# A chunked state-space scan beside a large projection: new state in three rounded products, state update first on VectorE, none of the scan on GpSimd

## The chip, the cores and the metric

The kernel runs on one core of one Trainium2 chip. The metric is the device time of one execution in microseconds (us); the kernel before was timed three times, and its median is 2664.36 us. About 0.2%, some 5 us, is what a timing of this kernel can tell from no change.

A core has several engines with instruction queues of their own: TensorE for matrix products (its weight loads are listed apart, as PEld), VectorE (DVE in the rows), ScalarE (ACT), GpSimd (POOL) and SyncE (SP), whose queue here issues the DMA transfers. Each engine works through its queue in order, and an instruction that has to wait holds up those behind it.

## The reference

One layer of a hybrid encoder on 2048 positions of width 1024, float32 throughout: RMSNorm, one input projection, two token mixers side by side (a gated short convolution and a Mamba-2 scan), an output projection with a residual, RMSNorm, a squared-ReLU MLP of width 4096 with a residual, and a last RMSNorm. The part that matters here is the scan:

```
x_c    = xs * dt                                  # per head
scores = einsum("bclgn,bcsgn->bclsg", c_c, b_c)
y_diag = einsum("bclsgr,bcsgrp->bclgrp", scores * decay, x_c)
states = einsum("bclgn,bclgrp->bcgrpn", b_c, x_c * decay_end)
h      = h_before * chunk_decay + states          # from chunk to chunk
y_off  = einsum("bclgn,bcgrpn->bclgrp", c_c, h_before) * exp(a_cum)
y      = rmsnorm_per_group((y_diag + y_off + d_skip * xs) * silu(z))
```

There are 16 heads of 64 in 2 groups, with a state of 128 per group.

## The kernel before

**Products.** Nearly all products are made of three products of rounded parts. A float32 array is split into `hi`, its copy rounded to the type fp32r, and `lo`, the rest (array minus `hi`, rounded as well); `mm3` issues whi·hi, whi·lo and wlo·hi into one PSUM bank. A split is a cast on ScalarE and a subtraction on VectorE (`split_w`, L100 and L101, for weights; L1422 and L1423 for the mixers' outputs). The small products of the scan are made in plain float32 instead; the trace has two records for each of these.

**Stages.** First the input projection runs on the first half of the positions, then on the second half; its products are `chain` (L276 to L278). From the second half on the scan runs as a side job: 32 chunks of 128 positions by one group (4 blocks of 512 positions, 2 groups, 4 chunks each), the first 16 beside the second half of the input projection and the last 16 beside the output projection. Then come the MLP and the last norm, which the change does not touch.

**The scan.** `Scan` gives each chunk a front and a back, generators whose steps `run` deals out. `front` transposes x and B (L1253, L1255) and makes the scores (L1256) on TensorE, copies the transposes out on ScalarE (L1258 `xtok`, L1260 `btok`), masks the scores (L1262), makes the decays on ScalarE (L1267, L1268), weights x by dt and by the decay to the end (`xdt` and `xde`, L1273) and multiplies decay by scores (L1275). `back` makes on TensorE the old state's part `yo` (L1287, 4 products), the new state `st` (L1289, one product of 512 columns) and the diagonal part `yd` (L1292, 8 products); then on VectorE `yo` times its decay (L1301), the state's decay (L1302), the addition of `st` to the state (L1303) and of `yd` (L1304); then on GpSimd the skip term (L1307) and the gate (L1308); then the group norm: squares on ScalarE (L1311), sums (L1312, L1314), a product with ones (L1317), a root (L1319), a reciprocal (L1320), a scaling (L1322), and the DMA to the scratch tensor `yn_d` (L1323).

**Buffers.** The two transposes, `st` and (in the first 16 chunks) the norm's sums take turns on two PSUM banks, tag "tp". So the transpose of B for the next chunk (`ptb`, L1255) takes the bank that `st` of this chunk had, and cannot start before L1303 has read it. `yo` and `yd` have a bank each. In the last 16 chunks the norm's sums take turns with the squares of the output projection (`sq`, L1491, read by L1492) on another single bank. `xtok` and `btok` have one buffer, `stmp` three in the first 16 chunks and four in the last.

**The output projection.** `Output` has 64 units; each is 24 products into one bank (L113 to L115), a residual addition on VectorE (L1478) and a DMA out (L1479). Units 0 to 31 use the short convolution's output, 32 to 47 the scan's output of blocks 0 and 1, 48 to 63 that of blocks 2 and 3, where block 3 is first used in unit 50. `schedule` lists at which half unit (`at` is 2n in the middle of unit n, 2n+1 at its end) a block of mixer output is fetched (L1408) and at which it is split into places (L1421 to L1423). The function `hook` runs in units 0 to 44 three steps of the scan a unit and whatever `todo` lists for that half unit. The scan's 134 steps are all dealt out when unit 44 ends. From unit 48 another `hook` deals out the preparation of the MLP's input.

**Order.** What is written is a priority, not the order on an engine: the framework plans every engine's queue with a model of durations, takes the first written instruction that its model says is ready, and fixes that order. In the trace L1302 comes before L1301 in some chunks and L1304 before L1303 in others. Instructions far ahead in the text run as soon as their data and buffers are there by the model.

Of the kernel before, what the change touches and what calls it, by code (L numbers as in the profile page):

```python
# [11 lines left out]
F32 = mybir.dt.float32  # L12
F32R = mybir.dt.float32r
AF = mybir.ActivationFunctionType
ALU = mybir.AluOpType

P = 128
# [22 lines left out]
def trunk(ctx: ExitStack, tc: tile.TileContext, x, w_in, w_dt, w_out, w_up, w_down, cvec, hrow, out):  # L40
    nc = tc.nc
# [38 lines left out]
        out=tri, in_=tri, compare_op=ALU.is_ge, fill=0.0, base=0, pattern=[[1, P]], channel_multiplier=-1  # L80
# [4 lines left out]
    def col(base, i):  # L85
        return cv[:, base + i : base + i + 1]
# [25 lines left out]
    def mm3(out, whi, wlo, hi, lo, k, nk):  # L112
        nc.tensor.matmul(out, whi, hi, start=(k == 0), stop=False)  # L113
        nc.tensor.matmul(out, whi, lo, start=False, stop=False)  # L114
        nc.tensor.matmul(out, wlo, hi, start=False, stop=(k == nk - 1))  # L115

    def psum(tag, name, bufs=1):
        if tag in turns:
            tag = next(turns[tag])
        return ps.tile([P, 512], F32, tag=tag, name=name, bufs=bufs)  # L120
# [1060 lines left out]
    class Scan:  # L1181
# [63 lines left out]
        def front(self, n):  # L1245

            b, g, c, h, ts, r0 = self.place(n)
            t = self.got[n]
            bT, cT = t["bc"][:, 0], t["bc"][:, 1]
            byhead = lambda a: a.rearrange("p (h d) -> p h d", h=HG)  # L1250
            pt = psum("tp", "ptx", 2)
            for j in range(4):
                nc.tensor.transpose(pt[:, j * P : (j + 1) * P], t["xd"][:, j], ident)  # L1253
            pb = psum("tp", "ptb", 2)
            nc.tensor.transpose(pb[:, 0:P], bT, ident)  # L1255
            nc.tensor.matmul(pb[:, P : 2 * P], bT, cT, start=True, stop=True)  # L1256
            xtok = self.tile([512], "xtok", 1)
            nc.scalar.copy(xtok, pt)  # L1258
            btok = t["btok"] = self.tile([P], "btok", 1)
            nc.scalar.copy(btok, pb[:, 0:P])  # L1260
            sm = self.tile([L], "smask", 1)
            nc.vector.tensor_tensor(out=sm, in0=pb[:, P : 2 * P], in1=tri, op=ALU.mult)  # L1262
            yield

            dec = t["dec"]
            for i in range(HG):
                nc.scalar.activation(dec[:, i], dec[:, i], AF.Relu, bias=t["a"][:, i : i + 1], scale=-1.0)  # L1267
            nc.scalar.activation(dec, dec, AF.Exp, scale=-1.0)  # L1268
            for j in range(4):
                nc.scalar.mul(t["xd"][:, j], t["xd"][:, j], col(C_D, 4 * g + j))  # L1270
            for k, by in (("xdt", "dt"), ("xde", "dend")):
                t[k] = self.tmp()
                nc.vector.tensor_tensor(out=byhead(t[k]), in0=byhead(xtok), in1=t[by], op=ALU.mult)  # L1273
            yield
            nc.vector.tensor_tensor(out=dec, in0=dec, in1=sm.unsqueeze(1).to_broadcast([P, HG, L]), op=ALU.mult)  # L1275
            yield

        def back(self, n):

            b, g, c, h, ts, r0 = self.place(n)  # L1280
            t = self.got.pop(n)
            cT = t["bc"][:, 1]
            byhead = lambda a: a.rearrange("p (h d) -> p h d", h=HG)
            state = self.state[g]
            yo = psum("k4", "yo")
            for j in range(4):
                nc.tensor.matmul(yo[:, j * L : (j + 1) * L], state[:, j * P : (j + 1) * P], cT, start=True, stop=True)  # L1287
            st = psum("tp", "st", 2)
            nc.tensor.matmul(st, t["btok"], t["xde"], start=True, stop=True)  # L1289
            yd = psum("k5", "yd")  # L1290
            for i in range(HG):
                nc.tensor.matmul(  # L1292
                    yd[(i % 2) * 64 : (i % 2) * 64 + 64, (i // 2) * L : (i // 2 + 1) * L],
                    byhead(t["xdt"])[:, i, :],
                    t["dec"][:, i, :],
                    start=True,
                    stop=True,
                )
            y = t["y"]
            t1 = self.tmp()  # L1300
            nc.vector.tensor_tensor(out=t1, in0=yo, in1=t["eb"].rearrange("p j l -> p (j l)"), op=ALU.mult)  # L1301
            nc.vector.tensor_tensor(out=byhead(state), in0=byhead(state), in1=t["cdec"], op=ALU.mult)  # L1302
            nc.vector.tensor_tensor(out=state, in0=state, in1=st, op=ALU.add)  # L1303
            nc.vector.tensor_tensor(out=t1, in0=t1, in1=yd, op=ALU.add)  # L1304
            yield
            t3 = t1.rearrange("p (j l) -> p j l", j=4)
            nc.gpsimd.tensor_tensor(out=t3, in0=t3, in1=t["xd"], op=ALU.add)  # L1307
            nc.gpsimd.tensor_tensor(out=y, in0=t3, in1=y, op=ALU.mult)  # L1308
            yield
            q4 = self.tmp().rearrange("p (j l) -> p j l", j=4)  # L1310
            nc.scalar.activation(q4, y, AF.Square)  # L1311
            nc.vector.tensor_tensor(out=q4[:, 0:2], in0=q4[:, 0:2], in1=q4[:, 2:4], op=ALU.add)  # L1312
            ssq = self.tile([L], "ssq", 1)
            nc.vector.tensor_tensor(out=ssq, in0=q4[:, 0], in1=q4[:, 1], op=ALU.add)  # L1314
            yield
            pss = psum("tp", "pss", 2) if self.bufs == 1 else psum("mw", "pss")
            nc.tensor.matmul(pss[:, 0:L], ones, ssq, start=True, stop=True)  # L1317
            r = self.tile([L], "srstd", 1)
            nc.scalar.activation(r, pss[:, 0:L], AF.Sqrt, bias=eps, scale=1.0 / 512)  # L1319
            nc.vector.reciprocal(out=r, in_=r)  # L1320
            yield
            nc.vector.tensor_tensor(out=y, in0=y, in1=r.unsqueeze(1).to_broadcast([P, 4, L]), op=ALU.mult)  # L1322
            nc.sync.dma_start(yn_d[h][:, 4 * g : 4 * g + 4, ts], y)  # L1323
            yield

        def run(self, begin, end):
# [10 lines left out]
            if self.bufs == 1:  # L1337
                for n in range(begin, end):
                    back = self.back(n)
                    front = self.front(n + 1) if n + 1 < end else iter(())  # L1340
                    next(back)
                    yield
                    next(back)
                    self.load(n + 1)
                    self.load_rows(n + 1)
                    yield
                    next(back)
                    yield
                    yield
                    next(front, None)  # L1350
                    yield
                    next(back)
                    yield
                    next(front, None)
                    yield
                    next(back)
                    self.load_gate(n + 1)
                    yield
                    next(front, None)
                    yield  # L1360
                return
# [28 lines left out]
    class Output:  # L1390
# [103 lines left out]
        def schedule(self):  # L1494

            self.todo = {}
            held = {}

            def put(i, b, c, load, splits):
                def fetch():  # L1500
                    held[i, b] = [self.fetch(i, b, k, self.raw) for k in range(0, KD, 2)]

                self.todo.setdefault(load, []).append(fetch)
                for j, at in enumerate(splits):
                    self.todo.setdefault(at, []).append(lambda j=j: self.fill(i, b, c, 2 * j, held[i, b][j]))

            put(0, 2, 2, 2, (5, 7, 9, 11))
            put(0, 3, 0, 26, (30, 30, 31, 31))
            put(1, 0, 1, 34, (38, 40, 42, 44))
            put(1, 1, 2, 58, (62, 62, 63, 63))  # L1510
            put(1, 2, 0, 68, (72, 74, 76, 78))
            put(1, 3, 1, 90, (94, 94, 95, 95))


    c4 = ctx.enter_context(ExitStack())
    with ExitStack() as c1:
# [7 lines left out]
        proj_out = Output(proj.places)  # L1524
# [10 lines left out]
        with ExitStack() as c2:  # L1535
            scan.open(c2, "sp2", 2)
            side = scan.run(len(CHUNKS) // 2, len(CHUNKS))

            def hook(at):
                for _ in range(1 + at % 2):  # L1540
                    next(side, None)
                for f in proj_out.todo.pop(at, ()):
                    f()

            for n in range(45):
                proj_out.unit(n, hook)
            for _ in side:
                pass
            for n in range(45, 48):
                proj_out.unit(n, hook)  # L1550
        c5.close()
        mlp = Mlp()
        mlp.raws = c4.enter_context(tc.tile_pool(name="ur", bufs=1, side="right", reuse_waits="tile"))
# [8 lines left out]

        def hook(at):
            next(late, None)
            if at == 2 * 61 + 1:
                mlp.settle(mlp.places, 0, [t[0] for t in mlp.held])

# [75 lines left out]
```

## Time and profile before

| | |
|---|---|
| timed runs | 2661.9, 2664.36 and 2666.43 us |
| the profiled execution's own time | 2658.11 us |
| its span | 2656.4 us |
| mean granted TensorE clock | 0.995 of full |
| busy: TensorE, weight loads | 2602.2 us, 2124.8 us |
| busy: VectorE, ScalarE, GpSimd | 1874.3 us, 1436.5 us, 146.1 us |
| scan's first 16 chunks | 470 to 980 us of the span, about |
| scan's last 16 chunks | 980 to 1295 us, about |

Busy time of TensorE counts pipelined products with ends that are modelled, so the cost of a product is read from start to start of the products around it, not from its own duration. Times in rows are from the start of the span. A row of an engine's idle time names what ended it.

### The profile page before, as it was taken

Reading aid. Unit: us, or ns where it says so; the run is one execution under the profiler, and the core shown is the slowest. Engines: PE = TensorE matmul, PEld = TensorE weight load, DVE = VectorE, ACT = ScalarE, POOL = GpSimd, SP = SyncE. Lnnn points to the kernel's source line nnn. Section 1 sums busy time; section 2 is a strip of 40 time slices with the busy share of each in tenths; the row PEclk is TensorE's granted clock in tenths of the full one; section 3 lists DMA queues with packets and bytes.
Section 4 is the critical chain, followed back from the end, with each engine's and each line's share of the span. In section 5 each row is a group of like instructions: output and inputs, shape, how many; then the busy total and the mean of one; then the engine's idle time right before and its main releaser. Section 6 shows DMA issues by size and latency. Waiting matters only on the chain.

```text
span 2656.4 us, 33528 instructions
## 1 busy us (share of the span) xinstructions
PE 2602.2 (98%) x12024; PEld 2124.8 (80%) x12024; DVE 1874.3 (71%) x2524; ACT 1436.5 (54%) x2178; POOL 146.1 (6%) x162
## 2 busy tenths in 40 slices
PE   7999999999999999998999999999999999999998
PEld 5788888778877888776888888888887888888887
DVE  7977867667667666666678675744447877888985
ACT  6654345766567566857336555755555434444443
POOL 0010000111111001111000000000000000000001
PEclk9999999999999999999999999999999999999999
DMA  3545735555555578867566786765558554665762
GB/s 145 196 174 182 278 143 202 182 152 174 169 161 168 165 262 267 254 200 232 193 208 214 258 315 254 258 234 178 209 183 297 155 152 153 206 219 165 249 209 71
DMA packets 292871, 536.96 MB, mean 202 GB/s; under 512 B 26208, under 2 KB 141920, under 8 KB 292704
## 3 DMA queue, kind: packets, MB, share of 16 engines
q1 hardware_dynamic: 292704, 534.82, 60.9%
q8 instruction: 94, 1.54, 0.2%
q14 instruction: 73, 0.60, 0.1%
HBM read 354.89 MB, written 179.83 MB: 201 GB/s over the span
## 4 chain that ended last, share of the span: by engine, by line
PE 59%; issue 26%; ACT 5%; DMA 4%; DVE 4%; POOL 1%; SPq 0%; POOLq 0%; DVEq 0%; ACTq 0%
PE px L276 9%; PE px L277 9%; PE px L278 9%; PE py L276 4%; PE py L277 4%; PE py L278 4%; PE pm L113 4%; PE pm L114 4%; PE pm L115 3%; PE pw L276 2%; PE pw L277 2%; PE pw L278 2%; ACT whi L100 1%; ACT dec L1267 1%; DMA dec<-rd_d 1%
## 5 line engine op out<-in xcount | busy, mean ns | idle before, releaser
L276 PE MATMUL px<-uh,whi 128*128 128x512 f32 x1672 | 657.7, 393 | 6.8 <-DVE acc L1018 1.8
L278 PE MATMUL px<-uh,wlo 128*128 128x512 f32 x1672 | 652.2, 390 | 0.0
L277 PE MATMUL px<-ul,whi 128*128 128x512 f32 x1672 | 651.9, 390 | 0.0
L276 PEld LDWEIGHTS px<-uh,whi 128*128 128x128 f32 x1672 | 314.5, 188 | 82.2 <-DVE acc L1018 3.2
L101 DVE TENSOR_TENSOR wlo<-wraw,whi 128x1024 fp32r<-128x1024 f32 x214 | 223.2, 1043 | 222.2 <-ACT whi L100 216.4
L278 PEld LDWEIGHTS px<-uh,wlo 128*128 128x128 f32 x1672 | 314.4, 188 | 66.4 <-issue 0.2
L277 PEld LDWEIGHTS px<-ul,whi 128*128 128x128 f32 x1672 | 314.6, 188 | 63.5
L100 ACT CAST whi<-wraw 128x1024 fp32r<-128x1024 f32 x214 | 193.6, 905 | 302.5 <-PE px L277 223.4
L276 PE MATMUL py<-uh,whi 128*128 128x512 f32 x836 | 327.4, 392 | 4.4 <-DVE acc L1018 3.4
L100 ACT CAST whi<-s 128x1024 fp32r<-128x1024 f32 x210 | 219.7, 1046 | 206.8 <-PE py L277 81.8
L277 PE MATMUL py<-ul,whi 128*128 128x512 f32 x836 | 325.6, 389 | 0.0
L278 PE MATMUL py<-uh,wlo 128*128 128x512 f32 x836 | 325.4, 389 | 0.0
L101 DVE TENSOR_TENSOR wlo<-s,whi 128x1024 fp32r<-128x1024 f32 x210 | 255.2, 1216 | 79.9 <-ACT whi L100 78.1
L113 PE MATMUL pm<-uh,whi 128*128 128x512 f32 (+1 forms) x648 | 253.1, 392 | 2.1 <-ACT uh L205 2.1
L114 PE MATMUL pm<-ul,whi 128*128 128x512 f32 (+1 forms) x648 | 249.9, 386 | 0.0
L115 PE MATMUL pm<-uh,wlo 128*128 128x512 f32 (+1 forms) x648 | 249.5, 385 | 0.0
L276 PEld LDWEIGHTS py<-uh,whi 128*128 128x128 f32 x836 | 156.9, 188 | 39.8 <-DVE acc L1018 3.8
L278 PEld LDWEIGHTS py<-uh,wlo 128*128 128x128 f32 x836 | 156.9, 188 | 33.0 <-DVE wlo L101 0.2
L277 PEld LDWEIGHTS py<-ul,whi 128*128 128x128 f32 x836 | 157.0, 188 | 32.0
L276 PE MATMUL pw<-uh,whi 128*128 128x512 f32 x418 | 163.5, 391 | 0.7 <-ACT pw L283 0.7
L347 ACT CAST uh<-rh 128x1024 fp32r<-128x1024 f32 (+1 forms) x128 | 120.3, 943 | 80.4 <-PE py L278 62.4
L278 PE MATMUL pw<-uh,wlo 128*128 128x512 f32 x418 | 162.9, 390 | 0.0
(232 smaller groups left out, 3763.2 us busy)
## 6 DMA issues: line engine op xcount, KB each, us to landing
hid_d<-e SPq DMA_DIRECT2D x96, 512.0 KB, 3.9
rh<-hid_d SPq DMA_DIRECT2D x96, 512.0 KB, 4.4
wraw<-w_in SPq DMA_DIRECT2D x68, 512.0 KB, 3.9
wraw<-w_down SPq DMA_DIRECT2D x104, 256.0 KB, 3.7
wraw<-w_up SPq DMA_DIRECT2D x48, 512.0 KB, 4.5
dec<-rd_d SPq DMA_DIRECT2D x32, 512.0 KB, 5.8
wraw<-w_out SPq DMA_DIRECT2D x32, 512.0 KB, 5.1
x_d<-xt SPq DMA_DIRECT2D x64, 256.0 KB, 3.2
```

Source lines behind the costliest of these rows:

```text
L100: nc.scalar.copy(hi, raw)
L101: eng.tensor_tensor(out=lo, in0=raw, in1=hi.bitcast(F32), op=ALU.subtract)
L113: nc.tensor.matmul(out, whi, hi, start=(k == 0), stop=False)
L114: nc.tensor.matmul(out, whi, lo, start=False, stop=False)
L115: nc.tensor.matmul(out, wlo, hi, start=False, stop=(k == nk - 1))
L276: nc.tensor.matmul(p, hi, h[0], start=not seeded and k == 0, stop=False, **kw)
L277: nc.tensor.matmul(p, hi, h[1], start=False, stop=False, **kw)
L278: nc.tensor.matmul(p, lo, h[0], start=False, stop=(k == len(g) - 1), **kw)
L347: nc.scalar.copy(p[i][0], t)
L1267: nc.scalar.activation(dec[:, i], dec[:, i], AF.Relu, bias=t["a"][:, i : i + 1], scale=-1.0)
```

## The change

1. **New state as three rounded products.** `btok` becomes a pair: `hi` is the old `btok` tile, now rounded, and `lo` overwrites B itself in its load buffer (a VectorE subtraction from PSUM). `xde` is split as well: `hi` goes into the `xtok` buffer (a ScalarE copy), `lo` into one more `stmp` buffer (a VectorE subtraction). `mm3` replaces the one float32 product.
2. **Order of the back.** `st` is written ahead of `yo` on TensorE. On VectorE the state's decay and addition are written ahead of `yo` times its decay.
3. **GpSimd's two operations go to VectorE**, in place.
4. **The end.** Block 3 of the scan's output is fetched at half unit 93 instead of 90 and split at 96, 97, 98 and 99 instead of 94, 94, 95 and 95, so that the second `hook` has to run `todo` too. The loop over units 0 to 44 becomes one over 0 to 47.

```
-            btok = t["btok"] = self.tile([P], "btok", 1)
-            nc.scalar.copy(btok, pb[:, 0:P])
+            hi, lo = t["btok"] = self.tile([P], "btok", 1).bitcast(F32R), bT.bitcast(F32R)
+            nc.scalar.copy(hi, pb[:, 0:P])
+            nc.vector.tensor_tensor(out=lo, in0=pb[:, 0:P], in1=hi.bitcast(F32), op=ALU.subtract)
...
-            yield
+            hi, lo = t["parts"] = [a.bitcast(F32R) for a in (self.tile([512], "xtok", 1), self.tmp())]
+            nc.scalar.copy(hi, t["xde"])
+            yield
+            nc.vector.tensor_tensor(out=lo, in0=t["xde"], in1=hi.bitcast(F32), op=ALU.subtract)
...
+            st = psum("tp", "st", 2)
+            mm3(st, *t["btok"], *t["parts"], 0, 1)
             yo = psum("k4", "yo")
...
-            st = psum("tp", "st", 2)
-            nc.tensor.matmul(st, t["btok"], t["xde"], start=True, stop=True)
...
-            nc.vector.tensor_tensor(out=t1, in0=yo, in1=t["eb"].rearrange("p j l -> p (j l)"), op=ALU.mult)
             nc.vector.tensor_tensor(out=byhead(state), in0=byhead(state), in1=t["cdec"], op=ALU.mult)
             nc.vector.tensor_tensor(out=state, in0=state, in1=st, op=ALU.add)
+            nc.vector.tensor_tensor(out=t1, in0=yo, in1=t["eb"].rearrange("p j l -> p (j l)"), op=ALU.mult)
...
-            nc.gpsimd.tensor_tensor(out=t3, in0=t3, in1=t["xd"], op=ALU.add)
-            nc.gpsimd.tensor_tensor(out=y, in0=t3, in1=y, op=ALU.mult)
+            nc.vector.tensor_tensor(out=t3, in0=t3, in1=t["xd"], op=ALU.add)
+            nc.vector.tensor_tensor(out=y, in0=t3, in1=y, op=ALU.mult)
...
-            put(1, 3, 1, 90, (94, 94, 95, 95))
+            put(1, 3, 1, 93, (96, 97, 98, 99))
...
-            for n in range(45):
+            for n in range(48):
                 proj_out.unit(n, hook)
             for _ in side:
                 pass
-            for n in range(45, 48):
-                proj_out.unit(n, hook)
...
         def hook(at):
             next(late, None)
+            for f in proj_out.todo.pop(at, ()):
+                f()
```

## The prediction

> **What bounds the kernel now.** I read the page's busy lines and its slices first, then the stages by window, then who waited for whom in the scan's second stage.
>
> ```profile
> PE 2602.2 (98%) x12024; PEld 2124.8 (80%) x12024; DVE 1874.3 (71%) x2524; ACT 1436.5 (54%) x2178; POOL 146.1 (6%) x162
> ...
> PE   7999999999999999998999999999999999999998
> ...
> 980.00:1295.00 315.00, 303.89 (x1592) 243.86 (x1591) 205.40 (x309) 202.35 (x402) 47.23 (x32) 0.98 0.79 233
> 470.00:980.00 510.00, 503.84 (x2481) 403.27 (x2480) 351.46 (x480) 333.81 (x564) 58.34 (x72) 1.00 0.55 174
> ```
>
> The columns of a window are its length, then busy time of PE, PEld, DVE, ACT and POOL, the granted clock, the DMA share and GB/s. TensorE bounds everything: the one slice of the middle that is not full is the 19th, in the scan's second stage, where 315.00 − 303.89 = 11.1 us are idle and the clock is 0.98. VectorE is busy 205.4 of 315 us there (65%) and 351.5 of 510 us (69%) in the first stage, so it is no bound, but it has work queued. So two things can change the time: how long TensorE's scan products take, and the waits of TensorE in the second stage. These are:
>
> ```profile
> PE pss L1317 <- DVE facc L1492: 5.4, 1, 5.4
> PE ptb L1255 <- DVE state L1303: 5.2, 3, 2.9
> PE st L1289 <- DVE stmp L1273: 0.4, 1, 0.4
> ```
>
> They hold nearly all of the 11.1 us: 5.4 in one wait of the norm's sums, 5.2 in three waits of a transpose of B for the bank of `st`.
>
> **Part 1, the product.** TensorE in the last chunk, in starts:
>
> ```profile
> 1273.98 0.39 PE L115 MATMUL pm<-uh,wlo 128*128 128x512 f32 x1
> 1274.20 0.39 PE L113 MATMUL pm<-uh,whi 128*128 128x512 f32 x1
> 1274.43 0.39 PE L114 MATMUL pm<-ul,whi 128*128 128x512 f32 x1
> 1274.66 0.39 PE L115 MATMUL pm<-uh,wlo 128*128 128x512 f32 x1
> ...
> 1275.78 1.02 PE L1289 MATMUL st<-stmp,btok 128*128 128x512 f32 x2
> 1276.73 1.09 PE L1292 MATMUL yd<-dec,stmp 128*64 128x128 f32 x16
> ```
>
> `st` holds TensorE from 1275.78 to 1276.73, 0.95 us. Three rounded products of the same shape hold it from 1273.98 to 1274.66, 0.68 us. That is 0.27 us a chunk, and 32 × 0.27 = **8.6 us** less on the engine that bounds. The third weight load hides, as the loads of the projection do (their 0.19 us lie inside 0.225). The gain lies between 0 and 8.6 us: if the planner puts `st` where its new `lo` isn't there yet, each chunk can give the 0.27 us back.
>
> The Trainium skill gives another price: FP8 and Floating Point Precision, TensorE Precision Notes, has a true float32 product make four passes, and TensorE: Matmul & The Clock Gate, Back-to-back issue gap, has a pass of 512 columns take 512/2.4 + 2.5 = 215.8 ns. One pass less is an estimate of 32 × 0.216 = 6.9 us; the row's 0.95 us is more than four such passes (0.86 us), so I keep the measurement.
>
> **Part 1, its splits, and part 3.** The nearest rows, by median:
>
> ```profile
> L1423 DVE TENSOR_TENSOR ul<-ry,uh x64: 678/685/1639, 953.8 to 1310.6; 128x512 fp32r<-128x512 f32 x64
> L1262 DVE TENSOR_TENSOR smask<-ptb,tri x32: 228/284/292, 479.8 to 1267.4; 128x128 f32<-128x128 f32 x32
> L1422 ACT CAST uh<-ry x64: 602/615/622, 953.1 to 1308.7; 128x512 fp32r<-128x512 f32 x64
> L1322 DVE TENSOR_TENSOR y<-y,srstd x32: 672/689/1773, 507.5 to 1293.9; 128x512 f32<-128x512 f32 x32
> L1307 POOL TENSOR_TENSOR stmp<-stmp,xd x32: 1277/1291/3335, 488.9 to 1279.8; 128x512 f32<-128x512 f32 x32
> L1308 POOL TENSOR_TENSOR y<-stmp,y x32: 1263/1291/1732, 491.1 to 1281.2; 128x512 f32<-128x512 f32 x32
> ```
>
> A chunk adds to VectorE 0.28 us (`lo` of B, the shape of L1262), 0.685 (`lo` of `xde`, as L1423) and 2 × 0.69 (skip term and gate, as L1322): 2.35 us, 75 us in all. ScalarE gets one cast of 0.615 us a chunk, 19.7 us in all; the copy of `btok` was there. GpSimd loses 2.58 us a chunk. With 16 × 2.35 = 37.6 us more VectorE comes to (205.4 + 37.6)/315 = 77% in the second stage and (351.5 + 37.6)/510 = 76% in the first. What hides this is TensorE's own queue: a unit's bank is read by VectorE while two other banks are filled, and weights are split two units ahead. What it doesn't hide from are the places where TensorE waits for the scan itself, the transpose after L1303 and now `st` after its `lo`. For these I take **2.5 us** more, against bounds of nothing and the rival below. No DMA is added or removed. In exchange the chain to the norm is shorter: y is there 2.58 − 1.38 = 1.2 us sooner, and the squares behind it on ScalarE (L1311), which hold up ScalarE's queue meanwhile.
>
> **Part 2, the order.** VectorE ahead of the longest of the three waits, which ended at 1219.3:
>
> ```profile
> 1215.63 0.69 DVE L1478 TENSOR_TENSOR xt<-pm,xt 128x512 f32<-128x512 f32 x1
> 1216.23 0.68 DVE L1301 TENSOR_TENSOR stmp<-yo,eb 128x512 f32<-128x512 f32 x1
> 1216.83 0.68 DVE L1302 TENSOR_TENSOR state<-state,dd 128x512 f32<-128x512 f32 x1
> 1217.42 1.22 DVE L101 TENSOR_TENSOR wlo<-wraw,whi 128x1024 fp32r<-128x1024 f32 x1
> 1218.56 0.68 DVE L1303 TENSOR_TENSOR state<-state,st 128x512 f32<-128x512 f32 x1
> ...
> 1215.00:1225.00 10.00, 7.08 (x29) 5.54 (x28) 9.47 (x15) 8.89 (x16) 2.79 (x2) 0.83 0.89 236
> ```
>
> With L1301 behind the state, L1302 and L1303 come 0.60 us sooner, by the step from 1216.23 to 1216.83. If L101 no longer falls between them, 1.14 us more. So each wait shrinks by 0.6 to 1.74 us: 3 × 0.6 = 1.8 us of the 5.2 at least, and at most 2.9 − 1.74 = 1.2 us are left of the longest and nothing of the others, 4.0 us gone. The clock adds to it. In the window with the 2.9 us wait it was 0.83, so 10 × 0.17 = 1.7 us are lost besides the wait, and a shorter wait may not cost them. I take **4 us** from a range of 0 (the planner moves the transpose forward by as much) to 5.7.
>
> Here the skill disagrees with the row: TensorE: Matmul & The Clock Gate, What's actually happening, gives the half rate after at least one idle window of about 3.4 us, and by that a 2.9 us wait would have cost no clock; the 0.83 says that it did, and by the page this part would lose its 1.7 us.
>
> **The other wait** (5.4 us) is no part of the diff, but lies behind what the diff shortens. The chain of waits ahead of it:
>
> ```profile
> 1223.49 0.60 DVE y L1322
> 1224.12 4.15 DMA yn_d<-y
> 1228.29 0.37 SPq L1243
> 1228.71 0.50 SPq L1408
> 1229.31 4.23 DMA xt<-x_d
> 1233.56 0.68 DVE facc L1492
> ...
> 1235.75 5.93 DMA dec<-rd_d
> 1241.76 0.40 ACT dec L1267
> 1242.16 0.50 ACT sq L1491
> ...
> 1240.00:1250.00 10.00, 6.58 (x26) 5.71 (x27) 4.46 (x9) 7.17 (x17) 0.00 (x0) 0.66 0.58 153
> ```
>
> The write of a chunk's y, begun after L1322, holds SP's queue 4.15 us because a fetch of block 3 (L1408) stands there early; later ScalarE's squares stand behind a decay whose transfer takes 5.93 us, and the norm's sums behind the squares. After the wait the clock is 0.66 over ten microseconds of which 6.58 are busy, some 6.58 × 0.34 = 2.2 us more. All 7.6 us may go when y comes 1.2 us sooner and the queues fall otherwise, or none, as the two transfers stay as long. I take **3 us**.
>
> **Part 4.** Half unit 93 is three half units of 24 × 0.2265/2 = 2.7 us after 90, 8.2 us. Before:
>
> ```profile
> 1297.52 0.37 SPq L1408 DMA_DIRECT2D ry<-yn_d  x1
> 1307.66 1.65 ACT L1422 CAST uh<-ry 128x512 fp32r<-128x512 f32 x3
> 1308.79 2.49 DVE L1423 TENSOR_TENSOR ul<-ry,uh 128x512 fp32r<-128x512 f32 x4
> 1311.80 0.68 DVE L1478 TENSOR_TENSOR xt<-pm,xt 128x512 f32<-128x512 f32 x1
> ```
>
> The splits end at 1311.3, as unit 47 ends (its addition is at 1311.80). Unit 50 starts two units (10.9 us) later, at about 1322.7. A shift of 8.2 us ends them at 1319.5, still ahead, and the fetch of the first half of this block at 1228.71, some 60 us ahead of half unit 90, shows that the place in the text hardly sets the time. So **0**, with units 48 and 49 as cover; if the splits came later than that, what is missing would be a wait of at most 3 us at unit 50. The loop to 48 changes nothing: all 134 steps of the scan are dealt out by unit 44.
>
> **The sum.** −8.6 − 4 − 3 + 2.5 + 0 = −13.1 us. The profiled execution took 2658.1 us by its own time (span 2656.4 and 1.7 around it), so 2645 by that; the median of the runs shown is 2664.4, 6.3 us longer, and against it the forecast is 2664.4 − 13.1 = **2651 us**.
>
> **The rivals.**
>
> *Every wait of the second stage goes*: −8.6 − 5.7 − 7.6 = −21.9, 2642 us. For it: both waits stand behind VectorE, and the diff moves the operations that end them forward. Against it: VectorE has 77% to do, and the decay's 5.93 us transfer isn't touched. Chance 0.17.
>
> *No change*: the planner keeps the distances. It places the transpose by its own durations, so a state that is ready sooner by the model lets it place the transpose sooner, and `st` right behind `lo` waits as the transpose did. The 8.6 us are eaten by 16 waits of 0.5 us in the second stage, 8 us: 2664 us. For it: orders in the trace already differ from the text. Against it: TensorE waited for `st` 0.4 us in all. Chance 0.21. That the rounded products don't run at the projection's 0.225 us is out, as it is the same form.
>
> *Slower: VectorE comes late to the bank of `st`.* In front of L1303 there are now the two `lo` of this chunk and, from the chunk before, skip term and gate: 2.35 us, less the 0.6 us of L1301. Where the queue has no gap, each of the second stage's 16 transposes waits up to 1.75 us more. It decides from 0.5 us a chunk on (16 × 0.5 = 8). At 1 us it costs 16, so −8.6 + 16 = +7.4, 2672 us, and more where a wait takes the clock down. For it: in the window 1215 to 1225 VectorE was busy 9.47 of 10 us already. Against it: 35% of the stage is free, and the operations removed from GpSimd held other queues up. Chance 0.17.
>
> The forecast has the rest, 0.45. The range is 2640 to 2668: below, all waits gone and some of the first stage's small ones; above, the slower case at 0.8 us a chunk, which leaves about half of it out. The likeliest case alone spans 2645 to 2658. Faster by over 0.2% (5.3 us): 0.45 + 0.17 = 0.62; within it 0.21; slower 0.17.
>
> **What would show it.** Part 1: `st` has 96 rounded products 0.225 us apart, and from its first to `yo` some 0.68 us. Part 2: the row of the transpose waiting for L1303 is gone or under 2 us. Part 3: GpSimd's two rows are gone, VectorE is near 1950 us, L1311 waits for VectorE less than for GpSimd before. Part 4: no TensorE wait near unit 50. Wrong it would be by TensorE waiting at `st` for `lo`, by the second stage's idle time above 11 us, or by a clock under 0.98 there.

## The result, and the profile after

The changed kernel takes 2651.32 us in the median (2649.23 to 2655.1), against 2663.64 us (2661.9 to 2666.43) of the kernel before beside it. The ratio is 0.9956, with a 95% interval of 0.9941 to 0.997: **11.7 us, or 0.44%, faster** (the two medians are 12.3 us apart). The forecast was 2651 us. The time is right; most of the terms behind it are not, and that is what the experiments are about.

The busy lines of the changed kernel, then its two scan stages (length, busy PE, PEld, DVE, ACT, POOL, granted clock, DMA share, GB/s):

```profile
PE 2597.8 (98%) x12056; PEld 2133.7 (81%) x12056; DVE 1926.7 (73%) x2652; ACT 1455.0 (55%) x2212; POOL 54.0 (2%) x98
...
PE   7999999999999999999999999999999999999998
```

```profile
470.00:980.00 510.00, 505.52 (x2526) 411.46 (x2525) 382.11 (x551) 348.14 (x593) 14.21 (x38) 1.00 0.58 177
980.00:1295.00 315.00, 305.68 (x1614) 250.42 (x1613) 230.39 (x369) 209.63 (x412) 0.00 (x0) 0.99 0.79 234
```

The profiled executions differ by less than the medians, 2656.4 to 2649.1 us of span, since the one of before was shorter than the median of its runs. The hole in the 19th slice has closed. The second stage has 315.00 − 305.68 = 9.3 us idle on TensorE (11.1 before), and 32 more instructions of TensorE than before take 4.4 us less. VectorE rose by 52 us, not by the 75 us that the added instructions come to by their durations. Part of that is only counting: neighbours on VectorE overlap (operations of 0.68 us start 0.60 us apart in the prediction's rows from 1215.63 on), and busy time counts an overlap once.

TensorE's waits in the scan, of the changed kernel (us in total, times, longest):

```profile
PE st L113 <- ACT xtok L1276: 8.1, 3, 4.5
...
PE st L114 <- DVE stmp L1278: 1.1, 3, 0.6
```

The two old waits, 5.4 us of the norm's sums for L1492 and 5.2 us of B's transpose for L1303, are gone. In their place stand 9.2 us at `st`: 8.1 us for `hi`, which ScalarE casts (L1276), and 1.1 us for `lo` (L1278). The longest of these waits, in order of time:

```profile
1216.86 1.28 ACT L1268 ACTIVATE dec<-dec,dd 128x128 f32<-128x128 f32 x4 [2.20 <-DMA dec<-rd_d]
...
1222.70 1.28 ACT L1269 ACT_TABLE_LOAD   x1
1224.00 1.06 ACT L1269 ACTIVATE dec<-dec 128x1024 f32<-128x1024 f32 x1
...
1224.96 0.60 ACT L1276 CAST xtok<-stmp 128x512 fp32r<-128x512 f32 x1
...
1225.61 0.79 PE L113 MATMUL st<-xtok,btok 128*128 128x512 f32 x1 [4.47 <-ACT xtok L1276]
1226.34 0.79 PE L114 MATMUL st<-stmp,btok 128*128 128x512 f32 x1
1226.93 0.63 PE L115 MATMUL st<-xtok,bc 128*128 128x512 f32 x1
```

The cast stands behind the decays in ScalarE's queue, and the decays had waited 2.20 us for their transfer. Right ahead of it stand the loading of a table for the exponential, 1.28 us, and the exponential of the decays itself (L1269). VectorE had `xde` ready at 1222.25, 2.7 us before the cast began. In the second longest of these waits, 2.53 us up to 1164.52, `xde` was ready as the wait began, and the same two instructions and the cast fill it. After the longest wait the three products start 0.73 and 0.59 us apart; undisturbed they are 0.23 apart. The 0.73 is one more wait, for `lo`, which VectorE had ready at 1226.29.

The last chunk shows the whole group of the scan's back without a wait:

```profile
1266.61 0.40 PE L113 MATMUL st<-xtok,btok 128*128 128x512 f32 x1
1266.84 0.40 PE L114 MATMUL st<-stmp,btok 128*128 128x512 f32 x1
...
1267.31 1.05 PE L1293 MATMUL yo<-bc,state 128*128 128x128 f32 x8
1268.29 1.09 PE L1296 MATMUL yd<-dec,stmp 128*64 128x128 f32 x16
1269.32 0.50 PE L113 MATMUL pm<-uh,whi 128*128 128x512 f32 x1
```

From the first of `st` to the next rounded product it is 1269.32 − 1266.61 = 2.71 us. The same group in the kernel before:

```profile
1274.89 1.05 PE L1287 MATMUL yo<-bc,state 128*128 128x128 f32 x8
...
1277.75 0.50 PE L113 MATMUL pm<-uh,whi 128*128 128x512 f32 x1
```

Here it is 2.86 us. So a chunk saves 0.15 us on TensorE, not 0.27. In undisturbed chunks of the first stage, where the input projection's products follow, the group goes from 2.87 to 2.69 us.

### The profile page after: what moved, and what is told of

Same layout as the page of the kernel before. It is cut to its first block, busy times and chain, and to the rows that moved or that the text cites. A ratio compares the mean times of both kernels' runs of the same rounds, so it can differ in the third digit from the quotient of the medians.

```text
span 2649.1 us, 33645 instructions
## 1 busy us (share of the span) xinstructions
PE 2597.8 (98%) x12056; PEld 2133.7 (81%) x12056; DVE 1926.7 (73%) x2652; ACT 1455.0 (55%) x2212; POOL 54.0 (2%) x98
## 4 chain that ended last, share of the span: by engine, by line
PE 61%; issue 25%; DMA 6%; ACT 5%; DVE 2%; SPq 0%; POOL 0%; POOLq 0%; DVEq 0%; ACTq 0%
PE px L276 9%; PE px L277 9%; PE px L278 9%; PE py L276 4%; PE py L278 4%; PE py L277 4%; PE pm L113 3%; PE pm L114 3%; PE pm L115 3%; DMA dec<-rd_d 3%; PE pw L276 2%; PE pw L278 2%; PE pw L277 2%; ACT dec L1268 1%; PE yd L1296 1%
```

## Experiments

Each is compared with the kernel before on the same chip; the ratio comes with its 95% interval, and 0.1% is 2.7 us. The four parts are those of the change: product, order, GpSimd's operations to VectorE, end.

### The changed kernel without part 1

The two splits are left out as well:

```
-            hi, lo = t["btok"] = self.tile([P], "btok", 1).bitcast(F32R), bT.bitcast(F32R)
+            btok = t["btok"] = self.tile([P], "btok", 1)
...
-            mm3(st, *t["btok"], *t["parts"], 0, 1)
+            nc.tensor.matmul(st, t["btok"], t["xde"], start=True, stop=True)
```

> The changed kernel with the new state again as one float32 product (no splits of B and xde; the order, VectorE's two operations and the end as changed). Theory A (the product is worth 0.27 us a chunk on TensorE, 8.6 us, and the wait of TensorE for the cast of xde takes some 9 us plus clock back): this is level with the changed kernel, within 3 us of 2651, with no wait at st and st 0.95 us from start to start. Theory B (the rounded products are worth nothing on the path, the gain came from the waits alone): this is faster than the changed kernel by the 9 us of its new waits, about 2641. Theory C (the product carries nearly all of the gain and the new waits cost little): this is back near 2660.

Measured: 0.9976 (0.9966 to 0.9985), where the whole change gave 0.9956. By the difference the product is worth 0.20% or some **5.3 us**, and the other three parts 0.24%. The two intervals just overlap, so this figure may be off by nearly as much as it is; the starts on TensorE, further down, give a sharper one. TensorE waits 3.4 us at `st` for `xde`, 3.0 us at B's transpose and 1.2 us at the norm's sums there. The result lies between theories A and C, and the 8.6 us that I had counted for the product are not there.

### xdt, xde and their cast written ahead of the decays

```
-            dec = t["dec"]
-            for i in range(HG): ...
             for k, by in (("xdt", "dt"), ("xde", "dend")): ...
             hi, lo = t["parts"] = ...
             nc.scalar.copy(hi, t["xde"])
+            dec = t["dec"]
+            for i in range(HG): ...
```

> The changed kernel with xdt, xde and the rounded copy of xde written ahead of the decays in the front, so that ScalarE's queue has that copy before the eight decays and their transfer. Theory A (TensorE's 8.1 us at st are the copy standing behind decays that wait for their transfer): the waits at st fall under 2 us and the time by 8 to 11 us, to about 2641. Rival (VectorE and ScalarE are late as a whole, and the place where TensorE notices only moves): the waits turn up at yd or at the transposes with the same sum, and the time stays within 3 us of 2651.

Measured: 0.9959 (0.9944 to 0.9973), the time of the changed kernel. The waits stayed; TensorE's waits and ScalarE's queue at one place of this run:

```profile
PE st L113 <- ACT xtok L1270: 7.7, 4, 2.9
```

```profile
1098.17 1.57 ACT L1273 ACTIVATE dec<-dec,dd 128x128 f32<-128x128 f32 x5 [2.91 <-DMA dec<-rd_d]
...
1103.46 0.61 ACT L1270 CAST xtok<-stmp 128x512 fp32r<-128x512 f32 x1
```

The planner still puts the decays (now L1273) ahead of the cast (now L1270), waiting for their transfer as before. So the experiment didn't do what it was made for: the written order is not the order on the engine.

### The product of the new state twice, before and after

```
             nc.tensor.matmul(st, t["btok"], t["xde"], start=True, stop=True)
+            nc.tensor.matmul(st, t["btok"], t["xde"], start=True, stop=True)
```

> The kernel before with the float32 product of the new state issued twice into the same bank, nothing else: what one such product costs on the path. Theory A, by the start-to-start time of 0.95 us: 32 x 0.95 = 30.4 us more, about 2694. Theory B (the product hides in TensorE's queue in part): 15 us more or less.

```
             mm3(st, *t["btok"], *t["parts"], 0, 1)
+            mm3(st, *t["btok"], *t["parts"], 0, 1)
```

> The changed kernel with the three rounded products of the new state issued twice, nothing else. Theory A: 32 x 0.68 = 21.8 us more than the changed kernel, about 2673, so that the two doublings differ by 8.6 us. Theory B: both doublings cost the same.

Measured: 1.0076 (1.0063 to 1.0089), 20 us more than the kernel before; and 1.0063 (1.0049 to 1.0077), 28 us more than the changed kernel by the two ratios. Forecast were 30.4 and 21.8 us; the two doublings differ the other way round. (By the spans of the two profiled executions, 2671.3 and 2649.1, the second is 22.2 us, but the first of these spans is of one of the shortest of its runs, 2673.43 us where their median is 2678.12.) The totals don't give a price of the product to a tenth of a microsecond, since waits move with them: with the first edit the transpose's waits for VectorE fell from 5.2 to 0.6 us. The starts on TensorE do give it. One chunk of each, first the kernel before with its product twice, then the second three of the changed kernel with its three twice:

```profile
1278.26 1.02 PE L1289 MATMUL st<-stmp,btok 128*128 128x512 f32 x2
1279.12 1.02 PE L1290 MATMUL st<-stmp,btok 128*128 128x512 f32 x2
1280.07 1.09 PE L1293 MATMUL yd<-dec,stmp 128*64 128x128 f32 x16
```

```profile
1268.66 0.40 PE L113 MATMUL st<-xtok,btok 128*128 128x512 f32 x1
...
1269.36 0.61 PE L1294 MATMUL yo<-bc,state 128*128 128x128 f32 x4
```

A float32 product followed by its like holds TensorE for 0.86 us; followed by `yd`, whose weights are 64 columns wide (128*64 in the rows), it is 0.95. So 0.09 us of the 0.95 belong to the hand-over to `yd`, and that is paid by whatever product stands in front of it. With part 2 alone (below) `yo` stands there:

```profile
1272.01 1.02 PE L1286 MATMUL st<-stmp,btok 128*128 128x512 f32 x2
1272.87 1.05 PE L1289 MATMUL yo<-bc,state 128*128 128x128 f32 x8
1273.85 1.09 PE L1292 MATMUL yd<-dec,stmp 128*64 128x128 f32 x16
```

The float32 `st` takes 0.86 us now, and `yo` 0.98, where it took 0.89 ahead of `st` (1274.89 to 1275.78 in the kernel before). Three rounded products take 0.70. The difference is 0.16 us a chunk, which agrees with the 2.86 − 2.71 of the whole groups: 32 × 0.16 = **5.1 us**, close to the 5.3 us of the run without part 1.

### Each part alone

Part 1 alone, with its two splits (order, GpSimd's operations and end as before):

```
-            nc.tensor.matmul(st, t["btok"], t["xde"], start=True, stop=True)
+            mm3(st, *t["btok"], *t["parts"], 0, 1)
```

> The kernel before with part 1 alone: splits of B and xde, three rounded products in the old place behind yo, all else as before. Theory A (on record): 8.6 us less TensorE work, and in sight of the waits of the changed kernel at st (9.2 us) and of the old waits at the transposes (5.2 us) and sums (5.4 us) standing: between no gain and -8.6, about 2655 against 2661. Rival (st in front is what makes the gain): no gain, 2661.

Part 2 alone:

```
+            st = psum("tp", "st", 2)
+            nc.tensor.matmul(st, t["btok"], t["xde"], start=True, stop=True)
             yo = psum("k4", "yo")
...
-            st = psum("tp", "st", 2)
-            nc.tensor.matmul(st, t["btok"], t["xde"], start=True, stop=True)
...
-            nc.vector.tensor_tensor(out=t1, in0=yo, in1=t["eb"].rearrange("p j l -> p (j l)"), op=ALU.mult)
...
             nc.vector.tensor_tensor(out=state, in0=state, in1=st, op=ALU.add)
+            nc.vector.tensor_tensor(out=t1, in0=yo, in1=t["eb"].rearrange("p j l -> p (j l)"), op=ALU.mult)
```

> The kernel before with part 2 alone: st (one float32 product) written ahead of yo, the state's two operations ahead of L1301. Theory A: the transposes' waits for the state fall from 5.2 us to under 1.5, 4 us less, about 2657, the 5.4 us wait stays. Rival (the planner keeps the distances): the same waits, within 2 us of 2661.

Part 3 alone:

```
-            nc.gpsimd.tensor_tensor(out=t3, in0=t3, in1=t["xd"], op=ALU.add)
-            nc.gpsimd.tensor_tensor(out=y, in0=t3, in1=y, op=ALU.mult)
+            nc.vector.tensor_tensor(out=t3, in0=t3, in1=t["xd"], op=ALU.add)
+            nc.vector.tensor_tensor(out=y, in0=t3, in1=y, op=ALU.mult)
```

> The kernel before with part 3 alone: skip term and gate on VectorE instead of GpSimd. Theory A: the squares on ScalarE come 1.2 us sooner, the 5.4 us wait at the norm's sums goes or halves, against more queue ahead of the state on VectorE: -3 us, about 2658. Rival (VectorE late): the waits at the transposes grow by 16 x 0.5 us or more, 2664 or over.

Part 4 alone, with the loop to 48 and the second `hook` that runs `todo`:

```
-            put(1, 3, 1, 90, (94, 94, 95, 95))
+            put(1, 3, 1, 93, (96, 97, 98, 99))
```

> The kernel before with part 4 alone: block 3 fetched at half unit 93 and split at 96 to 99. Theory A: nothing, within 2 us of 2661, the first half of the block still fetched some 60 us ahead. Rival: a wait of up to 3 us at unit 50, or, where the early fetch no longer holds SP's queue, up to 7 us less.

| part alone | ratio | 95% interval | about |
|---|---|---|---|
| product | 0.9986 | 0.9977 to 0.9996 | −3.7 us |
| order | 0.9999 | 0.9989 to 1.0009 | 0 |
| GpSimd's operations to VectorE | 0.9966 | 0.9952 to 0.9979 | −9.0 us |
| end | 0.9997 | 0.9987 to 1.0006 | 0 |

The four add up to −0.52%, the whole change has −0.44%, which is the same within the intervals. **The part I had priced at next to nothing is the bulk.** With part 3 alone TensorE's idle time in the two stages falls from 6.2 + 11.1 to 3.0 + 8.1 us; these 6.2 us are nearly all of the 6.8 by which its profiled execution is shorter (2656.4 to 2649.6). The order only moved a wait, as TensorE's waits with part 2 alone show:

```profile
PE st L1286 <- DVE stmp L1273: 4.3, 2, 2.5
PE pss L1317 <- DVE facc L1492: 4.2, 1, 4.2
PE ptb L1255 <- DVE state L1302: 2.8, 2, 1.9
```

The transpose waits 2.4 us less, and `st`, which waited 0.4 us before, waits 4.3 us for `xde`.

With part 3 alone, VectorE is busy 369.26 and 220.50 us in the two stages:

```profile
470.00:980.00 510.00, 506.97 (x2512) 407.10 (x2512) 369.26 (x519) 340.22 (x574) 15.97 (x38) 1.00 0.57 177
980.00:1295.00 315.00, 306.95 (x1600) 246.36 (x1599) 220.50 (x339) 202.72 (x399) 0.00 (x0) 0.99 0.79 235
```

Before it was 351.46 and 205.40 us, but the windows hold 69 more instructions now, not only the 64 added. Over the whole span, with 64 more, the durations of VectorE's instructions add up to 2048.3 us instead of 2015.8, 32.5 us more, though 64 operations of 0.685 us, 43.8 us, were added. So other VectorE work became 11 us shorter. The rows name it. In the kernel before, at one place (VectorE and GpSimd in order of time) and over all operations of L652:

```profile
528.88 3.21 DVE L652 SCALAR_TENSOR_TENSOR dts<-dts 128x64 f32<-128x64 f32 x4
529.10 1.28 POOL L1307 TENSOR_TENSOR stmp<-stmp,xd 128x512 f32<-128x512 f32 x1 [13.23 <-DVE dts L652]
...
530.46 1.29 POOL L1308 TENSOR_TENSOR y<-stmp,y 128x512 f32<-128x512 f32 x1
```

```profile
L652 DVE SCALAR_TENSOR_TENSOR dts<-dts x28: 213/220/1329, 62.4 to 531.9; 128x64 f32<-128x64 f32 x28
```

Four small operations of 0.22 us each take 3.21 us while GpSimd's two run. With part 3 alone the same 28 have no outlier:

```profile
L652 DVE SCALAR_TENSOR_TENSOR dts<-dts x28: 215/221/228, 61.7 to 530.2; 128x64 f32<-128x64 f32 x28
```

Behind such operations stood a wait of TensorE, `pc` (L662) for L656, 2.2 us in all before and 0.2 us with part 3 alone. It also goes the other way. In the kernel before:

```profile
1196.26 2.49 DVE L1423 TENSOR_TENSOR ul<-ry,uh 128x512 fp32r<-128x512 f32 x4
1196.58 3.33 POOL L1307 TENSOR_TENSOR stmp<-stmp,xd 128x512 f32<-128x512 f32 x1 [17.32 <-DVE stmp L1304]
```

Four subtractions in a row hold GpSimd's 1.29 us operation for 3.33 us, and y with it. Operations that read a PSUM bank besides SBUF (the on-chip memory of the engines) are not held: of the 32 L1303 in the kernel before 13 overlap an operation of GpSimd, and yet they have

```profile
L1303 DVE TENSOR_TENSOR state<-state,st x32: 677/681/691, 483.4 to 1279.5; 128x512 f32<-128x512 f32 x32
```

The Trainium skill says this in SBUF — State Buffer, SBUF: two separate sides: an operation of VectorE with two inputs from SBUF and one of GpSimd that reads SBUF exclude each other for the whole length of an instruction. The rows above agree with it.

### Part 3 with work given back to GpSimd

If the blocking is the cause, GpSimd work that nobody needs must bring the loss back. Part 3 alone, and two additions a chunk on GpSimd which overwrite x after its last use:

```
             nc.vector.tensor_tensor(out=y, in0=t3, in1=y, op=ALU.mult)
+            for _ in range(2):
+                nc.gpsimd.tensor_tensor(out=t["xd"], in0=t["xd"], in1=t["xd"], op=ALU.add)
```

> Part 3 alone (skip term and gate on VectorE), and after them two additions of the same size on GpSimd that only overwrite x, which nothing reads any more: GpSimd's load on the path to SBUF is back, the shorter chain to the squares stays. Theory D (part 3 gains because GpSimd's operations and VectorE's hold each other up): VectorE's operations of 0.22 and 0.685 us are again stretched to 1.3 us and more, and most of the 9 us is lost, 2657 or over. Theory E (part 3 gains because y is there 1.4 us sooner and ScalarE's queue is held less): the time stays within 3 us of 2651.

Measured: 1.0015 (1.0006 to 1.0024) against 0.9966 without the two additions: 13 us are back, slower than the kernel before. Its stages, and one place of it:

```profile
470.00:980.00 510.00, 503.29 (x2483) 402.60 (x2483) 378.89 (x513) 338.30 (x567) 61.69 (x70) 1.00 0.55 174
980.00:1295.00 315.00, 303.65 (x1585) 243.45 (x1584) 231.26 (x339) 201.91 (x402) 45.32 (x32) 0.98 0.78 231
```

```profile
530.40 2.52 POOL L1310 TENSOR_TENSOR xd<-xd 128x512 f32<-128x512 f32 x2 [14.12 <-DVE dts L652]
530.83 2.18 DVE L652 SCALAR_TENSOR_TENSOR dts<-dts 128x64 f32<-128x64 f32 x2
```

Over the whole span VectorE is busy 1928.3 us, 24.9 us more than the 1903.4 us with part 3 alone, for the same 2588 instructions: 0.39 us for each of the 64 GpSimd operations. TensorE's idle time in the two stages goes from 3.0 + 8.1 to 6.7 + 11.4 us, the clock of the second from 0.99 to 0.98, and TensorE's longest waits are now

```profile
PE ptb L1255 <- DVE state L1303: 5.0, 3, 2.8
PE ptx L1253 <- DMA xd<-xs_d: 3.2, 4, 1.4
PE st L1289 <- DVE stmp L1273: 3.0, 1, 3.0
PE pss L1319 <- DVE facc L1494: 2.4, 1, 2.4
```

The 3.2 us of x's transpose are a side effect of the edit, which holds x's buffer longer. If all of it is taken off, and it cost no more than its length, some 10 us of the 13 remain. Theory E is out as the main cause, since the chain to the squares stays as written in part 3 and the gain is gone; so most of what part 3 gains is blocking between GpSimd and VectorE that goes away. Which waits the blocking ends in is not fixed: `pc`, 2.2 us in the kernel before, stays at 0.4 here.

### What sets the wait at the new product

ScalarE's three copies (x's transpose, B's cast, the cast of `xde`) on VectorE, in the changed kernel:

```
-            nc.scalar.copy(xtok, pt)
+            nc.vector.tensor_copy(xtok, pt)
...
-            nc.scalar.copy(hi, pb[:, 0:P])
+            nc.vector.tensor_copy(hi, pb[:, 0:P])
...
-            nc.scalar.copy(hi, t["xde"])
+            nc.vector.tensor_copy(hi, t["xde"])
```

> The changed kernel with the three ScalarE operations ahead of st (the copy of the transposed x, the rounded copies of B and of xde) on VectorE: st no longer depends on ScalarE's queue, VectorE has about 1.65 us a chunk more. Theory F (TensorE waits at st because ScalarE's queue stands behind the decays' transfer): the waits at st fall from 9.2 to under 3 us and the time by 5 to 9 us, 2640 to 2644. Rival (VectorE has no room left): TensorE waits for VectorE instead, by as much or more, 2649 or over.

Measured: 0.9961 (0.9949 to 0.9974), again the changed kernel's time. The wait has changed the engine it is put down to:

```profile
PE st L113 <- DVE xtok L1276: 5.5, 2, 4.9
PE st L114 <- DVE stmp L1278: 2.8, 4, 1.1
```

But VectorE itself stood still ahead of the longest of these waits (4.9 us, up to 1221.68), for squares on ScalarE that stood behind decays:

```profile
1213.74 1.87 ACT L1268 ACTIVATE dec<-dec,dd 128x128 f32<-128x128 f32 x6 [3.80 <-DMA dec<-rd_d]
...
1216.62 0.58 ACT L1495 ACTIVATE sq<-xt 128x512 f32<-128x512 f32 x1
...
1217.23 0.69 DVE L1496 TENSOR_TENSOR facc<-sq,facc 128x512 f32<-128x512 f32 x1 [4.17 <-ACT sq L1495]
```

So moving the copies didn't take ScalarE's queue off this path, and the run doesn't speak against theory F.

Half of the decays' transfer, in the changed kernel (the decays of the other four heads are made from the first four's rows):

```
-            nc.sync.dma_start(t["dec"], rd_d[b][r0 : r0 + HG, 0, :].partition_broadcast(P))
+            nc.sync.dma_start(t["dec"][:, 0 : HG // 2], rd_d[b][r0 : r0 + HG // 2, 0, :].partition_broadcast(P))
...
-            for i in range(HG):
-                nc.scalar.activation(dec[:, i], dec[:, i], AF.Relu, bias=t["a"][:, i : i + 1], scale=-1.0)
+            for i in (4, 5, 6, 7, 0, 1, 2, 3):
+                nc.scalar.activation(dec[:, i], dec[:, i % 4], AF.Relu, bias=t["a"][:, i : i + 1], scale=-1.0)
```

> The changed kernel with half of the decays' transfer: the rows of four heads are loaded instead of eight, and the other four heads use them too, so that part of the computation (four heads' decays) is left out; all instructions of the engines stay. Theory F: ScalarE waits less for this transfer (28 us or so before), TensorE's waits at st for the cast fall from 8.1 to under 3 us, and the time by 5 to 9 us. Rival: no change at st, within 3 us of 2649.

Measured: 0.9986 (0.9978 to 0.9995), slower than the changed kernel. ScalarE waits 65.0 us in 18 waits for this transfer, in the changed kernel 43.9 us in 19 (not the 28 of the expectation). From issue to landing the transfer takes 4.7 us, not half of the 5.7 in the changed kernel. TensorE's waits at `st` are 6.5 us for `hi` and 1.1 for `lo`, and 3.1 us at the norm's sums are back. Half the bytes, and more waiting. A reading that fits, but that no run separates, is that the planner counts on the shorter transfer and puts the decays earlier in ScalarE's queue. The experiment doesn't decide whether the decays set the wait at `st`.

The changed kernel with the back's order as before, on VectorE too:

```
-            st = psum("tp", "st", 2)
-            mm3(st, *t["btok"], *t["parts"], 0, 1)
             yo = psum("k4", "yo")
...
+            st = psum("tp", "st", 2)
+            mm3(st, *t["btok"], *t["parts"], 0, 1)
```

> The changed kernel with part 2 undone: yo ahead of st on TensorE, yo's decay ahead of the state on VectorE. Theory G (part 2 gives nothing, as alone, and st in front costs cover): yo's 0.9 us go ahead of st, so each of the waits at st is up to 0.9 us shorter, 2 to 4 us faster than the changed kernel, 2645 to 2648, with the transposes' waits under 2 us. Rival (part 2 is what keeps the transposes from waiting once VectorE has more to do): the waits at the transposes come back, 2651 or over.

Measured: 0.9965 (0.9953 to 0.9978), where the change has 0.9956 (0.9941 to 0.997): no difference that can be told. TensorE waits 5.5 + 1.8 us at `st` and 3.3 us at the norm's sums, about as much as in the changed kernel. None of these versions is clearly faster than the changed kernel.

## Why the prediction was right, and where it was wrong

The total was forecast at −13.1 us and came out at −11.7. That is luck, by errors which cancel: the product was taken some 3.4 us too high and the order 4 us, GpSimd's operations some 8.5 us too low.

**Part 1, the product: right mechanism, size off.** The term "That is 0.27 us a chunk, and 32 × 0.27 = 8.6 us" failed. It set the distance from `st` to `yd`, 0.95 us with a hand-over in it, against the distance of three rounded products in the middle of their like, 0.68 without one. Measured over the whole group, 2.86 to 2.71, it is 0.15 to 0.16 us, 5 us in all; taken out of the changed kernel it is 5.3 us, alone 3.7. The group was there to be read in the trace of before, and the change left `yo` and `yd` in it. In the Trainium skill's FP8 and Floating Point Precision, TensorE Precision Notes, the float32 product makes four passes; with the 215.8 ns of a pass in TensorE: Matmul & The Clock Gate, Back-to-back issue gap, that is an estimate of 0.863 us, and the doubled product's 0.86 agrees. The estimate of 6.9 us that I put aside for the 0.95 was the nearer one.

**"The places where TensorE waits ... now `st` after its `lo`": right place, wrong operand.** `lo` costs 1.1 us of waits. The other half, `hi`, costs 8.1 us; in the longest of these waits ScalarE's queue had the decays, their transfer, a table load and the exponential in front of it. I had written ScalarE's cast down as 19.7 us of busy time and not asked what is queued ahead of it. The 2.5 us that I charged were too few for these waits; they are about as long as those that went (10.6 us), so the account of waits alone comes out near nothing.

**Part 2, the order: wrong.** I took 4 us; alone it gives nothing (0.9999), and taking it out again makes no difference that can be told. The step that failed is "each wait shrinks by 0.6 to 1.74 us" as a gain of TensorE. The transposes' waits did shrink, 5.2 to 2.8 us with the order alone, but TensorE then waited for the next thing. That is the second rival's mechanism, holding for this part and not for the whole.

**Part 3, GpSimd's operations: wrong, far too small.** I charged 2.5 us of waits for all that VectorE gets more to do (2.35 us a chunk, 1.38 of it for this part) and credited 3 us for a y that comes sooner, a net of −0.5. It gives −9.0 us alone. Whether the credit was well placed is not shown: the norm's sums wait 2.4 us instead of 5.4 with part 3 alone, but with part 1 alone, GpSimd's operations as they were, they wait 1.3. What was missing is that VectorE and GpSimd hold each other up. Rows that the prediction itself quotes said so: maxima of 1773 ns beside a median of 689 in L1322, and of 3335 beside 1291 in L1307. I read the medians only. VectorE's added work was thereby cheaper than its price, 32.5 us instead of 43.8 for this part.

**Part 4: right.** Alone it gives nothing (0.9997), and in the changed kernel TensorE is busy for all of the 30 us from 1310 to 1340, the stretch of unit 50.

**The slower rival** didn't come. It had VectorE late to the bank of `st`; in the changed kernel no transpose of B waits for that bank. Its condition, a queue without a gap, was judged on VectorE's busy time of before, which held time in which VectorE was only blocked: in its window from 1215 to 1225 that was one subtraction of 1.64 us instead of 0.69 (at 1221.85). VectorE came to 73% of the second stage (230.39 of 315), not to the 77% forecast.

**The signs I had named.** The products of `st` are 0.23 us apart, GpSimd's two rows are gone, the second stage is idle 9.3 us at a clock of 0.99, and ScalarE's squares (L1315) wait 24.8 us for VectorE, where they waited 106.5 us for GpSimd. VectorE is at 1926.7 us, under the 1950 I gave. One of the signs of being wrong did show, TensorE waiting for `lo`, with 1.1 us. By the other signs alone every part would have looked right; only the single parts showed otherwise.

**What stays open.** What sets the 9 us at `st` is not settled: neither the written order nor the engine of the casts removed them, and neither edit took ScalarE's queue of decays out of the path. How much of the 13 us with GpSimd's idle additions is blocking, and how much the later loads of x, is not measured by itself; the wait for x is 3.2 us. The changed kernel is 28 us longer with its product doubled, where 32 × 0.70 = 22.4 us were added on TensorE, and the kernel before 20 us, where it was 32 × 0.86 = 27.5; what moved besides is not traced.

## What to carry to other kernels

Price a replaced product on the whole run of instructions around it, from the last one ahead to the first one behind, since a hand-over between kinds of product stays whichever stands there. Look at the maximum beside the median of every VectorE row while GpSimd works: a long tail is time that leaves with GpSimd's operations, and here moving them to a VectorE with 30% free cost less than their duration and gained more than their latency. In these queues, planned ahead, a wait that was taken from one instruction turned up at another, so add up all waits of the stage before crediting one.

## What the runs showed of the hardware

- VectorE operations with both inputs in SBUF and GpSimd operations stopped each other: 0.22 us became up to 1.33 us (L652), 1.29 us became 3.33 us (L1307), and 64 GpSimd operations on 128 by 512 elements cost VectorE 24.9 us. Operations with an input in PSUM (L1303: 681 ns median, 691 at most, 13 of 32 beside GpSimd) were not touched.
- A float32 product of 128 by 128 by 512 held TensorE 0.86 us ahead of its like or of `yo` and 0.95 us ahead of `yd`, whose weights are 64 columns wide.
- TensorE ran at half rate after some waits of a few microseconds. In the kernel before, behind the 2.92 us wait at the transpose:

```profile
1219.30 0.33 PE L1255 MATMUL ptb<-ident,bc 128*128 128x128 f32 x1 [2.92 <-DVE state L1303]
...
1219.94 0.63 PE L114 MATMUL pm<-ul,whi 128*128 128x512 f32 x1
1220.37 0.63 PE L115 MATMUL pm<-uh,wlo 128*128 128x512 f32 x1
```

The starts are 0.43 us apart, where 0.225 is the rule of this stage. So a wait at this place costs more than its length. The length alone doesn't decide: the 1.94 us wait with part 2 alone (up to 1215.26) was followed by products 0.43 us apart as well, the 2.53 us wait of the changed kernel (up to 1164.52) was not.
